# A hybrid decoder layer: a partial sum of squares on VectorE, and tokens made one by one, in the opening

## The chip, the core and the metric

The kernel runs on one core of a Trainium2 chip. The metric is the device time of one execution in microseconds. The core has TensorE (PE in the profile; its weight loads are PEld), VectorE (DVE), ScalarE (ACT), GpSimd (POOL) and SyncE (SP), which here issues the loads and stores.

## The reference

One layer: adaLN modulation, a mixer (sliding-window attention beside a Mamba-2 scan), a SwiGLU network, float32, 2048 positions of width 1024. The opening of the kernel computes only what stands here, for the first 512 positions:

```python
mod = jax.nn.silu(c) @ w_ada[layer] + b_ada[layer]
shift1, scale1, gate1, shift2, scale2, gate2 = jnp.split(mod, N_MOD, axis=-1)
h = modulate(rmsnorm(x, norm1_w[layer]), shift1, scale1)   # h * (1 + scale) + shift
proj = h @ w_in                                            # here: the q, k, v and dt columns
```

## The kernel before, in words

The width of 1024 lies on the partitions as 8 blocks of 128, called d or k. A tile of x, `x0[d]`, is 128 (one block of the width) by 512 (positions). The positions are worked in four blocks of 512. "Token d" below is the finished operand h[d] of the first block, a pair of tiles: a high part rounded to fp32r, made on ScalarE, and a low part, the rest, made on VectorE. A weight tile is split in the same way, and a product of the two is three matmuls (`mm3`, L286 to L288).

`opening()` makes the first block's operands and its projections to queries (all 512 positions) and to keys, values and dt (256 positions).

- Sum of squares (L1376, L1378): ScalarE squares each `x0[d]`, TensorE multiplies each square by ones and adds over d in one bank, 4 matmuls of two columns per d, 32 in all. The page counts each f32 matmul as two instructions.
- Root and spread: `root_of` computes 1/rms per position on VectorE in twelve small steps, `diagonal` (L331) puts it on four diagonals, and the matmul in `spread` (L337) copies it to all partitions, into the bank `bc`.
- Modulation: for most d the two numbers per partition (scale, shift) come from rows of `w_ada`: two loads of 512 KB (`rows_of`) and two reduces on VectorE against `csil` (L1395), then `scl1` (L1398). For two of the d they come from TensorE: eight products of the silu of c with blocks of `w_ada` (`ada_loads`, `ada_products`, L175), copied by ScalarE as one line and turned into columns by small matmuls (`ada_columns`, L180 to L186).
- `pair_ready(kp, raws)`: makes two tokens and the three split weights (two for the queries, one for keys, values and dt) of one pair kp of blocks d. L1416 scales on VectorE, L1418 and L1423 are the token's high and low part, L1413, L1420, L1422 and L1424 those of the weights.
- `first_columns(h)` is a generator: each `next(main)` issues the 30 matmuls of one k.
- `silu_rows` and `silu_columns` make silu(c) as rows (`csil`) and as columns (`ccol`); `rope_angles` and `rope_tables` make the cosines and sines of the first block.

The whole of `opening()` stands in a `manual_schedule` for TensorE, VectorE, SyncE and ScalarE: these queues take its instructions in the order of the text. What follows is ordered by a planner at build time, which may queue an instruction of the following text between those of the opening, wherever it finds it ready. That holds for L1474 to L1476: the exponential `neg_a` on ScalarE, which needs the small load `row`, and two VectorE steps. The low parts of the next weights (L279) are held behind the opening's last VectorE instruction (`pair_done`).

Behind the opening come `drain(main)` (rotary embedding of what `first_columns` summed: L402 to L405, dt at L482), the keys and values of the other 256 positions, then the convolutions (L499 to L514) and the norm of the second block (`norm1`, L341 to L344, L368).

Buffers that matter here: 5 raw weight tiles (`RAW`) and 6 split ones (`SPLIT`), 8 temporaries (`TMP`), four row tiles in each of `common.m4` and `extra.m4`, four banks `dense()` and four side banks.

Of the kernel before, what the change touches and what calls it, by code (L numbers as in the profile page):

```python
# [12 lines left out]
F32 = mybir.dt.float32  # L13
# [32 lines left out]
def hymba_layer(ctx, tc, xT, xtok, pos, wada, wadk, vecs, rows, wq, wkv, wz, wx, wo, wgu, wd, outT):  # L46
# [24 lines left out]
    def side_bank(i):  # L71
        return bank(("am", "at", "sm", "st")[i], 1)

    def tmp():
        return big("t", TMP, pool=fw)
# [70 lines left out]
    csil = const([P, D], "csil", pool=ip)  # L146

    def silu_rows():
        for i in range(2):
            dg, bk = tmp(), side_bank(i)  # L150
            for j in range(4):
                nc.vector.tensor_scalar(dg[:, j * P:(j + 1) * P], ident, ccol[:, 4 * i + j:4 * i + j + 1], 0.0,
                                        ALU.mult, ALU.add)
            nc.tensor.matmul(bk, ones, dg, start=True, stop=True)
            nc.scalar.copy(csil[:, i * T:(i + 1) * T], bk)

    def silu_columns():
        th = tmp()[:, 0:KT]
        nc.scalar.activation(th, ccol, AF.Tanh, scale=0.5)
        nc.vector.scalar_tensor_tensor(ccol, th, 1.0, ccol, ALU.add, ALU.mult)  # L160
# [1202 lines left out]
    def opening():  # L1363
        h, x0 = [], []
        for d in range(KT):
            x = extra.m2()
            x0.append(x)
            nc.sync.dma_start(x, xT[0, d])
        silu_columns()
        silu_rows()  # L1370
        nc.vector.tensor_copy(posf, posi)
        angles = rope_angles(0, NT)
        st = side_bank(2)
        for d in range(KT):
            sq = tmp()
            nc.scalar.activation(sq, x0[d], AF.Square)  # L1376
            for t in range(NT):
                nc.tensor.matmul(st[:, 2 * t:2 * t + 2], sq[:, t * P:(t + 1) * P], ones[:, 0:2], start=d == 0 and t == 0,  # L1378
                                 stop=d == KT - 1 and t == NT - 1, skip_group_check=True)
        rope_tables(angles)  # L1380

        def fetched(kp):
            raws = [wt.tile([P, 528], F32, name="raw", tag="raw", bufs=RAW)[:, 0:n] for n in (T, T, 528)]
            for raw, src in zip(raws, (wq[0][kp], wq[1][kp], wkv[kp])):
                fetched.last = nc.sync.dma_start(raw, src)
            return raws

        def rows_of(d, tile):
            got = [tile().rearrange("p h t -> p (h t)").bitcast(F32) for _ in range(2)]
            for w, i in zip(got, (8 + d, d)):  # L1390
                nc.sync.dma_start(w, wada[i])
            return got

        def reduced(i, w):
            nc.vector.tensor_tensor_reduce(w, w, csil, 0.5, b_ada[:, i:i + 1], ALU.mult, ALU.add, mod[:, i:i + 1])  # L1395

        def scale_of(d):
            nc.vector.scalar_tensor_tensor(scl1[:, d:d + 1], mod[:, 8 + d:9 + d], 1.0, n1w[:, d:d + 1],  # L1398
                                           ALU.add, ALU.mult)

        def vectors(d, rows):
            reduced(8 + d, rows[0])
            reduced(d, rows[1])
            scale_of(d)

        def pair_ready(kp, raws):

            ds, ws, xs = (2 * kp, 2 * kp + 1), [], []
            for raw in raws:
                two = wt.tile([P, 2, 528], F32R, name="w", tag="w", bufs=SPLIT)  # L1410
                ws.append((two[:, 0, 0:raw.shape[1]], two[:, 1, 0:raw.shape[1]]))
            for i in range(2):
                nc.scalar.activation(ws[i][0], raws[i], AF.Copy)  # L1413
            for d in ds:
                x = tmp()
                nc.vector.scalar_tensor_tensor(x, x0[d], scl1[:, d:d + 1], bc, ALU.mult, ALU.mult)  # L1416
                h.append(operand())
                nc.scalar.activation(h[d][0], x, AF.Identity, bias=sh1[:, d:d + 1])  # L1418
                xs.append(x)
            nc.scalar.activation(ws[2][0], raws[2], AF.Copy)  # L1420
            for i, d in enumerate(ds):
                nc.vector.tensor_tensor(ws[i][1], raws[i], ws[i][0].bitcast(F32), ALU.subtract)  # L1422
                nc.vector.scalar_tensor_tensor(h[d][1], xs[i], sh1[:, d:d + 1], h[d][0].bitcast(F32), ALU.add, ALU.subtract)  # L1423
            last = nc.vector.tensor_tensor(ws[2][1], raws[2], ws[2][0].bitcast(F32), ALU.subtract)  # L1424
            pair_done[0] = last
            first_ws.append(ws)

        rows0, rows1 = rows_of(0, common.m4), rows_of(1, common.m4)
        nc.sync.dma_start(row, rows.broadcast_to([P, 32]))
        raws = [fetched(0)]  # L1430
        spare = []
        for _ in range(4):
            taken[0] += 1
            spare.append(ip.tile([P, 2, T], F32R, name="hl0", tag="hl0", bufs=4).bitcast(F32))
        first = ada_loads(0, spare)
        rows4, rows5 = rows_of(4, extra.m4), rows_of(5, extra.m4)
        line = side_bank(0)
        reduced(8, rows0[0])
        bc = spread(root_of(st, NT), bc=side_bank(1))
        reduced(0, rows0[1])  # L1440
        scale_of(0)
        ada_products(first, line, range(8))
        vectors(1, rows1)
        main = first_columns(h)
        pair_ready(0, raws[0])
        raws.append(fetched(1))
        rows6, rows7 = rows_of(6, common.m4), rows_of(7, common.m4)
        next(main)
        vectors(4, rows4)
        vectors(5, rows5)  # L1450
        ada_columns(line, side_bank(0), 2)
        next(main)
        pair_ready(1, raws[1])
        raws.append(fetched(2))
        next(main)
        next(main)
        pair_ready(2, raws[2])
        raws.append(fetched(3))
        next(main)
        next(main)  # L1460
        vectors(6, rows6)
        vectors(7, rows7)
        pair_ready(3, raws[3])
        next(main)
        next(main)
        return h, main, fetched.last

# [292 lines left out]
def _layout(x, c, positions, w_ada, b_ada, norm1_w, w_in, conv_w, conv_b, dt_bias, a_log, d_skip, attn_sinks,  # L1760
            ssm_norm_w, w_out, norm2_w, w_gate_up, w_down, final_norm_w):
    a = np.ascontiguousarray
    out = {}
    out["xT"] = a(x[0].T.reshape(KT, P, NB, T).transpose(2, 0, 1, 3))
    out["xtok"] = a(x[0].reshape(S // P, P, 2, T).transpose(0, 2, 1, 3))
    out["pos"] = a(positions[0].reshape(S // P, P).T)
    out["wada"] = a(w_ada[0].T.reshape(48, P, D))
    wk = w_ada[0].reshape(D, 6, 4, 2 * P)
    out["wadk"] = a(np.stack([np.concatenate([wk[:, 1, 1], wk[:, 0, 1]], axis=1)])
                    .reshape(1, 4, 2, P, T).transpose(0, 1, 3, 2, 4).reshape(1, 4, P, 2 * T))  # L1770
    cols = lambda v, n: v.reshape(n, P).T
    cw = conv_w[0].reshape(4, 8, P).transpose(2, 1, 0).reshape(P, 32)
    out["vecs"] = a(np.concatenate([cols(b_ada[0], 48), cols(norm1_w[0], 8), cols(norm2_w[0], 8),
                                    cols(final_norm_w, 8), cw, cols(conv_b[0], 8), cols(ssm_norm_w[0], 4), cols(c[0], 8)], axis=1))
    sk = attn_sinks[0].reshape(2, 4).T.reshape(8)
    out["rows"] = a(np.concatenate([dt_bias[0], a_log[0], d_skip[0], sk])[None])
    w = w_in[0]
    q = w[:, 0:512].reshape(D, 2, 4, 64).transpose(0, 2, 1, 3).reshape(D, 512)

    def moving(m, n):  # L1780
        return m.reshape(4, 2, P, -1, n).transpose(3, 0, 2, 1, 4).reshape(-1, 4, P, 2 * n)

    out["wq"] = a(moving(q, 256))
    out["wkv"] = a(moving(np.concatenate([w[:, 512:768], w[:, 2304:2312]], axis=1), 264)[0])
    out["wz"] = a(moving(w[:, 768:1280], 256))

    def chunks(m, n):
        return m.reshape(2, 4, P, n, P).transpose(3, 0, 2, 1, 4).reshape(n, 2, P, 512)

    out["wx"] = a(chunks(w[:, 1280:2304], 8))  # L1790
    wo = w_out[0]
    attn = wo[0:512].reshape(2, 4, 64, D).transpose(1, 0, 2, 3).reshape(512, D)
    out["wo"] = a(chunks(np.concatenate([attn, wo[512:]], axis=0), 8))
    gu = w_gate_up[0]
    out["wgu"] = a(np.stack([chunks(gu[:, :FF], NF), chunks(gu[:, FF:], NF)], axis=1))
    out["wd"] = a(w_down[0].reshape(KP, 2, P, 8, P).transpose(3, 1, 2, 0, 4).reshape(8, 2, P, KP * P))
    return out
# [20 lines left out]
```

## Time and profile before

| | |
|---|---|
| median of 3 runs | 2178.56 us (2177.98 to 2180.01) |
| profiled execution | 2179.79 us, span 2177.7 us |
| mean granted TensorE clock | 0.997 |
| TensorE, VectorE, ScalarE, GpSimd busy | 98%, 76%, 47%, 25% |
| DMA | 466.76 MB, mean 214 GB/s |

A busy time is the share of the span in which the engine had an instruction of the program at work; a wait is idle time and what ended it. TensorE's matmuls overlap, so its costs are read from start to start.

### The profile page before, as it was taken

Reading aid. Unit: us, or ns where it says so; the run is one execution under the profiler, and the core shown is the slowest. Engines: PE = TensorE matmul, PEld = TensorE weight load, DVE = VectorE, ACT = ScalarE, POOL = GpSimd, SP = SyncE. Lnnn points to the kernel's source line nnn. Section 1 sums busy time; section 2 is a strip of 40 time slices with the busy share of each in tenths; the row PEclk is TensorE's granted clock in tenths of the full one; section 3 lists DMA queues with packets and bytes.
Section 4 is the critical chain, followed back from the end, with each engine's and each line's share of the span. In section 5 each row is a group of like instructions: output and inputs, shape, how many; then the busy total and the mean of one; then the engine's idle time right before and its main releaser. Section 6 shows DMA issues by size and latency. Waiting matters only on the chain.

```text
span 2177.7 us, 33314 instructions
## 1 busy us (share of the span) xinstructions
PE 2139.7 (98%) x10984; PEld 1764.9 (81%) x10984; DVE 1651.1 (76%) x3195; ACT 1016.5 (47%) x2137; POOL 553.5 (25%) x658
## 2 busy tenths in 40 slices
PE   8989999999999999999999999999999999999998
PEld 6889898879778777788888878788888888888887
DVE  6987857885778866798897678777877765886576
ACT  3675735653557454433344445433333334554441
POOL 0223433322112211243441212333333331210011
PEclk9999999999999999999999999999999999999999
DMA  7798978797998332333335778645555536778553
GB/s 269 237 341 297 353 260 312 255 342 238 360 357 313 109 97 92 121 109 124 115 94 178 248 244 293 216 155 187 166 167 179 168 112 232 239 266 278 184 161 105
DMA packets 287708, 466.76 MB, mean 214 GB/s; under 512 B 27440, under 2 KB 97072, under 8 KB 287536
## 3 DMA queue, kind: packets, MB, share of 16 engines
q1 hardware_dynamic: 286960, 464.13, 63.3%
q8 instruction: 86, 1.41, 0.3%
q14 instruction: 86, 0.70, 0.1%
q10 hardware_dynamic: 576, 0.52, 0.1%
HBM read 329.73 MB, written 134.81 MB: 213 GB/s over the span
## 4 chain that ended last, share of the span: by engine, by line
PE 79%; DVE 8%; DMA 5%; ACT 3%; issue 2%; POOL 1%; SPq 0%; DVEq 0%; ACTq 0%; POOLq 0%
PE d L1182 17%; PE d L1052 9%; PE d L1051 9%; PE d L1050 9%; PE d L286 4%; PE d L287 4%; PE d L288 4%; DMA aw<-in_wada_dram 1%; PE d L1323 1%; PE am L1050 1%; PE am L1052 1%; PE am L1051 1%; PE am L706 1%; PE sm L1052 1%; PE sm L1051 1%
## 5 line engine op out<-in xcount | busy, mean ns | idle before, releaser
L1182 PE MATMUL d<-a,w 128*128 128x512 f32 x1716 | 403.5, 396 | 2.2 <-DVE a L1164 2.2
L1182 PEld LDWEIGHTS d<-a,w 128*128 128x128 f32 x1716 | 323.2, 189 | 79.6 <-DVE a L1164 2.9
L1052 PE MATMUL d<-b,w 128*128 128x512 f32 x924 | 366.9, 399 | 0.6 <-DVE w L898 0.6
L1051 PE MATMUL d<-b,w 128*128 128x512 f32 x924 | 366.6, 397 | 0.7 <-DVE b L932 0.5
L1050 PE MATMUL d<-b,w 128*128 128x512 f32 x924 | 363.2, 397 | 0.0
L897 ACT ACTIVATE w<-s 128x512 fp32r<-128x512 f32 x176 | 111.0, 631 | 237.2 <-PE d L1052 148.2
L1051 PEld LDWEIGHTS d<-b,w 128*128 128x128 f32 x924 | 174.2, 189 | 41.7 <-DVE b L932 1.5
L1052 PEld LDWEIGHTS d<-b,w 128*128 128x128 f32 x924 | 173.8, 188 | 40.4 <-DVE w L898 1.0
L1050 PEld LDWEIGHTS d<-b,w 128*128 128x128 f32 x924 | 174.2, 189 | 38.0
L286 PE MATMUL d<-w,hl 128*128 128x256 f32 (+1 forms) x592 | 171.9, 290 | 2.7 <-DVE s L511 2.7
L287 PE MATMUL d<-w,hl 128*128 128x256 f32 (+1 forms) x592 | 166.9, 282 | 0.0
L288 PE MATMUL d<-w,hl 128*128 128x256 f32 (+1 forms) x592 | 166.8, 282 | 0.0
L1178 DVE TENSOR_TENSOR w<-raw,w 128x512 fp32r<-128x512 f32 x156 | 114.0, 739 | 43.3 <-ACT w L1177 43.0
L1104 POOL TENSOR_TENSOR t<-t 128x512 f32<-128x512 f32 x44 | 75.5, 1717 | 277.0 <-DVE t L1103 126.1
L1164 DVE TENSOR_TENSOR a<-a 128x512 fp32r<-128x512 f32 x154 | 106.2, 704 | 46.1 <-ACT a L1163 45.3
L898 DVE TENSOR_TENSOR w<-s,w 128x512 fp32r<-128x512 f32 x176 | 131.1, 746 | 6.3 <-ACT w L897 5.4
L1163 ACT ACTIVATE a<-a 128x512 fp32r<-128x512 f32 x154 | 96.1, 629 | 85.1 <-DMA a<-act_t 50.1
L296 POOL TENSOR_TENSOR acc<-acc,t 128x512 f32<-128x512 f32 x35 | 51.8, 1481 | 325.7 <-ACT t L295 312.1
L286 PE MATMUL d<-hl,w 128*128 128x512 f32 x320 | 131.6, 411 | 0.0
L288 PE MATMUL d<-hl,w 128*128 128x512 f32 x320 | 126.1, 394 | 0.0
L1177 ACT ACTIVATE w<-raw 128x512 fp32r<-128x512 f32 x156 | 90.6, 587 | 75.8 <-PE d L1182 44.3
L287 PE MATMUL d<-hl,w 128*128 128x512 f32 x320 | 125.7, 393 | 0.0
(426 smaller groups left out, 4802.6 us busy)
## 6 DMA issues: line engine op xcount, KB each, us to landing
raw<-in_wgu_dram SPq DMA_DIRECT2D x176, 256.0 KB, 3.0
act_t<-t SPq DMA_DIRECT2D x88, 256.0 KB, 2.9
a<-act_t SPq DMA_DIRECT2D x88, 256.0 KB, 4.5
act_b<-t SPq DMA_DIRECT2D x66, 256.0 KB, 2.0
a<-act_b SPq DMA_DIRECT2D x66, 256.0 KB, 4.2
aw<-in_wada_dram SPq DMA_DIRECT2D x64, 256.0 KB, 5.1
w<-w_x SPq DMA_DIRECT2D x32, 512.0 KB, 5.5
raw<-wd_s SPq DMA_DIRECT2D x64, 256.0 KB, 3.2
```

Of the source, the lines that this page charges most:

```text
L286: nc.tensor.matmul(out, ahi, bhi, start=first, stop=False)
L287: nc.tensor.matmul(out, ahi, blo, start=False, stop=False)
L288: mm3.last = nc.tensor.matmul(out, alo, bhi, start=False, stop=last)
L897: nc.scalar.activation(hi, x, AF.Copy)
L898: eng.tensor_tensor(lo, x, hi.bitcast(F32), ALU.subtract)
L1050: nc.tensor.matmul(out, ahi, bhi, start=first and k == 0, stop=False, skip_group_check=True)
L1051: nc.tensor.matmul(out, ahi, blo, start=False, stop=False, skip_group_check=True)
L1052: mm3.last = nc.tensor.matmul(out, alo, bhi, start=False, stop=k == 3, skip_group_check=True)
L1163: nc.scalar.activation(hi, raw, AF.Copy)
L1164: nc.vector.tensor_tensor(lo, raw, hi.bitcast(F32), ALU.subtract)
L1178: nc.vector.tensor_tensor(w[1], raw, w[0].bitcast(F32), ALU.subtract)
L1182: mm3.last = nc.tensor.matmul(ps, w[x][:, ws], act[k][y], start=new and k == 0 and x + y == 0, stop=k == KP - 1 and x == 1, skip_group_che ...
```

## The change

- Sums: the squares of blocks 0, 1 and 2 go to TensorE as before. The square of block 3 is written into an accumulator tile, VectorE adds those of 4 to 7 to it, and TensorE sums the accumulator: 16 matmuls instead of 32.
- The two copies that end `silu_rows` are issued behind the squares of blocks 2 and 4.
- Loads: all of the opening's first loads are issued ahead of `silu_columns`. Behind x come the four blocks for the products, rows 0, the small `row`, the weights of pair 0, rows 3, two of the three weights of pair 1, rows 4 and 5; the third weight of pair 1 and rows 6 follow token 0.
- The products serve blocks 1 and 2 (before: 2 and 3); rows serve 0 and 3 to 7. Four products stand ahead of the spread, four behind it. `ada_columns` stands ahead of the first `next(main)`.
- Tokens: `pair_ready` is gone; `scaled_token` (scaling and high part), `closed` (low part), `high` and `low` (weights) stand one by one behind the reduces of their own rows.

```diff
     def silu_rows():
+        copies = []
...
-            nc.scalar.copy(csil[:, i * T:(i + 1) * T], bk)
+            copies.append(lambda i=i, bk=bk: nc.scalar.copy(csil[:, i * T:(i + 1) * T], bk))
+        return copies
...
+        early = ada_loads(0, spare)
+        rows0 = rows_of(0, common.m4)
+        nc.sync.dma_start(row, rows.broadcast_to([P, 32]))
+        raw0 = fetched(0)
+        rows3 = rows_of(3, extra.m4)
+        raw1 = fetched(1, (0, 1))
+        rows4, rows5 = rows_of(4, extra.m4), rows_of(5, common.m4)
+
+        silu_columns()
+        copies = silu_rows()
+        nc.vector.tensor_copy(posf, posi)
+        angles = rope_angles(0, NT)
+        st, acc = side_bank(2), sums()
...
+        for d in range(KT):
+            sq = acc if d == 3 else tmp()
+            nc.scalar.activation(sq, x0[d], AF.Square)
+            if d in (2, 4):
+                copies[d // 2 - 1]()
+            if d < 3:
+                summed(sq, d == 0, False)
+            elif d > 3:
+                nc.vector.tensor_tensor(acc, acc, sq, ALU.add)
+        rope_tables(angles)
+        summed(acc, False, True)
+
         line = side_bank(0)
-        reduced(8, rows0[0])
-        bc = spread(root_of(st, NT), bc=side_bank(1))
-        reduced(0, rows0[1])
-        scale_of(0)
-        ada_products(first, line, range(8))
-        vectors(1, rows1)
+        dg = diagonal(root_of(st, NT))
+        ada_products(early, line, range(4))
+        bc = spread(None, bc=side_bank(1), dg=dg)
+        ada_products(early, line, range(4, 8))
+        vectors(0, rows0)
+        w0 = high(raw0)
+        low(raw0, w0, (0,))
+        x = scaled_token(0)
+        low(raw0, w0, (1, 2))
+        closed(*x)
+        raw1 += fetched(1, (2,))
+        rows6 = rows_of(6, common.m4)
+        first_ws.append(w0)
+        vectors(3, rows3)
         main = first_columns(h)
-        pair_ready(0, raws[0])
-        raws.append(fetched(1))
-        rows6, rows7 = rows_of(6, common.m4), rows_of(7, common.m4)
+        ada_columns(line, side_bank(0), 1)
         next(main)
-        vectors(4, rows4)
-        vectors(5, rows5)
-        ada_columns(line, side_bank(0), 2)
-        next(main)
-        pair_ready(1, raws[1])
-        raws.append(fetched(2))
+
+        xs = [scaled_token(d) for d in (1, 2)]
+        w1 = high(raw1)
+        closed(*xs[0])
+        low(raw1, w1, (0,))
+        closed(*xs[1])
+        low(raw1, w1, (1, 2))
+        raw2, rows7 = fetched(2), rows_of(7, extra.m4)
+        first_ws.append(w1)
         next(main)
         next(main)
-        pair_ready(2, raws[2])
-        raws.append(fetched(3))
+
+        x = scaled_token(3)
+        vectors(4, rows4)
+        closed(*x)
         next(main)
+        x = scaled_token(4)
+        w2 = high(raw2)
+        low(raw2, w2, (0,))
+        closed(*x)
+        low(raw2, w2, (1, 2))
+        raw3 = fetched(3)
+        first_ws.append(w2)
         next(main)
+        vectors(5, rows5)
+        x = scaled_token(5)
         vectors(6, rows6)
+        closed(*x)
+        next(main)
+        x = scaled_token(6)
+        w3 = high(raw3)
+        low(raw3, w3, (0,))
+        closed(*x)
+        low(raw3, w3, (1, 2))
+        first_ws.append(w3)
+        next(main)
         vectors(7, rows7)
-        pair_ready(3, raws[3])
-        next(main)
+        closed(*scaled_token(7))
         next(main)
```

More of the change, by code (lines that the diff above doesn't have):

```diff
@@ L1368, in opening, with fetched @@
             nc.sync.dma_start(x, xT[0, d])
[L1369 to L1385, printed above, removed]
+        def fetched(kp, which=(0, 1, 2)):
+            raws = [wt.tile([P, 528], F32, name="raw", tag="raw", bufs=RAW)[:, 0:(T, T, 528)[i]] for i in which]
+            for raw, i in zip(raws, which):
+                fetched.last = nc.sync.dma_start(raw, (wq[0], wq[1], wkv)[i][kp])
             return raws
@@ L1392, in rows_of, with vectors, high @@
             return got
-        def reduced(i, w):
-            nc.vector.tensor_tensor_reduce(w, w, csil, 0.5, b_ada[:, i:i + 1], ALU.mult, ALU.add, mod[:, i:i + 1])
-        def scale_of(d):
+        def vectors(d, loaded):
+            for w, i in zip(loaded, (8 + d, d)):
+                nc.vector.tensor_tensor_reduce(w, w, csil, 0.5, b_ada[:, i:i + 1], ALU.mult, ALU.add, mod[:, i:i + 1])
             nc.vector.scalar_tensor_tensor(scl1[:, d:d + 1], mod[:, 8 + d:9 + d], 1.0, n1w[:, d:d + 1],
                                            ALU.add, ALU.mult)
[L1401 to L1408, printed above, removed]
+        def high(raws):
+            ws = []
             for raw in raws:
@@ L1411, in pair_ready, with low, scaled_token, closed @@
                 ws.append((two[:, 0, 0:raw.shape[1]], two[:, 1, 0:raw.shape[1]]))
[L1412 to L1430, printed above, removed]
+                nc.scalar.activation(ws[-1][0], raw, AF.Copy)
+            return ws
+        def low(raws, ws, which):
+            for i in which:
+                pair_done[0] = nc.vector.tensor_tensor(ws[i][1], raws[i], ws[i][0].bitcast(F32), ALU.subtract)
+        def scaled_token(d):
+            x = tmp()
+            nc.vector.scalar_tensor_tensor(x, x0[d], scl1[:, d:d + 1], bc, ALU.mult, ALU.mult)
+            hl = operand()
+            nc.scalar.activation(hl[0], x, AF.Identity, bias=sh1[:, d:d + 1])
+            return d, x, hl
+        def closed(d, x, hl):
+            pair_done[0] = nc.vector.scalar_tensor_tensor(hl[1], x, sh1[:, d:d + 1], hl[0].bitcast(F32),
+                                                          ALU.add, ALU.subtract)
+            h.append(hl)
         spare = []
@@ L1434, in opening @@
             spare.append(ip.tile([P, 2, T], F32R, name="hl0", tag="hl0", bufs=4).bitcast(F32))
-        first = ada_loads(0, spare)
-        rows4, rows5 = rows_of(4, extra.m4), rows_of(5, extra.m4)
-        line = side_bank(0)
-        reduced(8, rows0[0])
-        bc = spread(root_of(st, NT), bc=side_bank(1))
-        reduced(0, rows0[1])
-        scale_of(0)
-        ada_products(first, line, range(8))
-        vectors(1, rows1)
+        early = ada_loads(0, spare)
+        rows0 = rows_of(0, common.m4)
@@ new lines, in opening, with summed @@
+        nc.sync.dma_start(row, rows.broadcast_to([P, 32]))
[8 more added lines that the diff above has]
+        st, acc = side_bank(2), sums()
+        def summed(sq, first, last):
+            for t in range(NT):
+                nc.tensor.matmul(st[:, 2 * t:2 * t + 2], sq[:, t * P:(t + 1) * P], ones[:, 0:2], start=first and t == 0,
+                                 stop=last and t == NT - 1, skip_group_check=True)
@@ L1767, in _layout @@
     out["wada"] = a(w_ada[0].T.reshape(48, P, D))
-    wk = w_ada[0].reshape(D, 6, 4, 2 * P)
-    out["wadk"] = a(np.stack([np.concatenate([wk[:, 1, 1], wk[:, 0, 1]], axis=1)])
+    wk = w_ada[0].reshape(D, 6, D)[:, :, P:3 * P]
+    out["wadk"] = a(np.stack([np.concatenate([wk[:, 1], wk[:, 0]], axis=1)])
                     .reshape(1, 4, 2, P, T).transpose(0, 1, 3, 2, 4).reshape(1, 4, P, 2 * T))
```

## The prediction

> **What bounds the kernel now.** I read the page first, then the waits of TensorE, then the stretch up to 130 us in order of time, engine by engine, and last the loads with their landings.
>
> ```profile
> PE 2139.7 (98%) x10984; PEld 1764.9 (81%) x10984; DVE 1651.1 (76%) x3195; ACT 1016.5 (47%) x2137; POOL 553.5 (25%) x658
> ```
>
> TensorE is busy for 98% of the span, so only what shortens its work or its idle time moves the end. Of its waits in the first 110 us the view has three; this is the one the change touches most:
>
> ```profile
> PE at L337 <- DVE t L331: 3.3, 1, 3.3
> ```
>
> The opening in order of time (start, length, engine, line, tiles, count). Consecutive instructions overlap, so I take a cost from start to start.
>
> ```profile
> 8.95 4.26 ACT L1376 ACTIVATE t<-m 128x512 f32<-128x512 f32 x8
> 9.47 0.23 DVE L241 TENSOR_SCALAR m<-m 128x128 f32<-128x128 f32 x1
> 9.64 13.81 PE L1378 MATMUL sm<-ones,t 128*128 128x2 f32 x64 [1.21 <-ACT t L1376]
> 17.08 0.17 DVE L1475 TENSOR_SCALAR neg_a<-neg_a 128x8 f32<-128x8 f32 x1 [3.63 <-ACT neg_a L1474]
> 23.49 0.16 DVE L309 TENSOR_SCALAR ms<-sm 128x4 f32<-128x4 f32 x1 [6.24 <-PE sm L1378]
> 25.86 0.87 DVE L331 TENSOR_SCALAR t<-ident,rstd 128x128 f32<-128x128 f32 x4
> 26.79 2.07 PE L337 MATMUL at<-t,ones 128*128 128x512 f32 x2 [3.34 <-DVE t L331]
> 28.79 7.95 PE L175 MATMUL am<-hl,vec 128*1 128x512 f32 x16
> 36.67 0.39 PE L286 MATMUL d<-w,hl 128*128 128x256 f32 x1
> 36.83 0.58 ACT L180 COPY t<-am 1x512 f32<-1x512 f32 x1 [3.73 <-PE am L175]
> 40.45 1.05 PE L182 MATMUL am<-ones,t 1*128 1x2 f32 x8
> 41.43 0.39 PE L286 MATMUL d<-w,hl 128*128 128x256 f32 x1
> 46.40 1.39 DVE L1416 SCALAR_TENSOR_TENSOR t<-m,scl,at 128x512 f32<-128x512 f32 x2
> 50.87 1.27 DVE L1395 CUSTOM_DVE_ANT_0 m<-m,csil,vec 128x1024 f32<-128x1024 f32 x1
> 55.84 1.39 DVE L1416 SCALAR_TENSOR_TENSOR t<-m,scl,at 128x512 f32<-128x512 f32 x2
> 60.30 1.32 DVE L279 TENSOR_TENSOR w<-raw,w 128x528 fp32r<-128x528 f32 x2
> 66.63 0.28 PE L287 MATMUL am<-w,hl 128*128 128x264 f32 x1
> ```
>
> The reader sees one chain: squares, sums on TensorE (13.8 us), root and diagonal on VectorE, the spread, eight products L175, and at 36.67 the first projection matmul. From there TensorE never waits: token-row 0 takes 36.67 to 40.45, the column turn L182 1.0, and the other seven run from 41.43 to 66.63, 25.2/7 = 3.6 us each. VectorE ends the opening at 60.30. Its rates: two tokens with one weight pair take 50.87-46.40 = 4.47 us, two modulation rows with their scales 55.84-50.87 = 4.97 divided by two, 2.49 for one d (two reduces and a scale).
>
> **The change, part by part.**
>
> *Sums.* 64 instructions in 13.81 us are 0.216 each. Tokens 0 to 2 stay, and the accumulator is a fourth: 32 instead of 64, 6.9 us of TensorE removed. The squares go ahead of the two silu copies, so the sums can start when TensorE's silu products end (8.4, where the 1.2 us idle time before 9.64 began). Three rows of sums take 5.2 us, to 13.6.
>
> *The adds.* VectorE adds four squares into the fifth. The last x lands late:
>
> ```profile
> m<-in_xT_dram SPq DMA_DIRECT2D x1, 256.0 KB, 5.7
> L1422 DVE TENSOR_TENSOR w<-raw,w 128x512 fp32r<-128x512 f32 x8 | 5.5, 683 | 0.0
> L1423 DVE SCALAR_TENSOR_TENSOR hl<-t,mod,hl 128x512 fp32r<-128x512 f32 x8 | 5.9, 743 | 0.0
> L296 POOL TENSOR_TENSOR acc<-acc,t 128x512 f32<-128x512 f32 x35 | 51.8, 1481 | 325.7 <-ACT t L295 312.1
> ```
>
> Issued at 5.0, it lands at 10.7; its square (0.53 each by 4.26/8) is done at 11.3. VectorE is through with the angles at 9.7 (L241), so three adds fit ahead of that square and one follows. An f32 add of this shape stands on VectorE in no row of the opening; I take 0.68 by L1422, its nearest row, and bound it by nothing and by GpSimd's 1.48. So the accumulator is ready at 12.2, before TensorE wants it at 13.6; at 1.48 each, four from 9.7, it would be 15.6 and the sums would end 1.9 us later. With 0.68 they end at 13.6+1.7 = 15.4 against 23.45: 8 us earlier. An add that cost nothing would gain nothing, since TensorE is busy until 13.6.
>
> *The clock of the sums.* The loads of the sums are slow from first to last:
>
> ```profile
> L1378 PEld LDWEIGHTS sm<-ones,t x64: 288/333/333, 9.6 to 23.0; 128*128 128x128 f32 x64
> ```
>
> So I keep 0.216 for what remains. The Trainium skill ("TensorE: Matmul & The Clock Gate", Part 1) says that sustained work of some 3.4 us doubles the array's rate. By it the removed 32 would be worth 32 x 0.108 = 3.5 us, and the whole sum below 3.5 instead of 6.9. The row contradicts it for matmuls of two columns: 13 us of them without a pause, and the median load is the longest one. So the sum goes by the row.
>
> *Spread and products.* Root and diagonal take 23.49 to 26.79, 3.3 us: done at 18.7. Four products, moved ahead of the spread, fill that time, if their blocks have landed (below: 13.3). Half of L175's 7.95 and L337's 2.07 put the spread's end at 21.4, the other half the last product's at 25.4. TensorE's 3.3 us wait goes.
>
> *The column turn* is moved ahead of the first tokens: ScalarE's copy (0.58), covered before by token 0's matmuls, is now bare, then L182's 1.0: first projection matmul at 27.0, 9.7 us earlier, and the 1.0 that stood between tokens 0 and 1 is gone. Token 0 would end at 30.6, and with VectorE keeping up TensorE would be 10.7 us ahead. VectorE does not keep up, as its walk below shows.
>
> *Loads.* The queue and two landings (from issue):
>
> ```profile
> 5.51 2.92 SPq L1391 DMA_DIRECT2D m<-in_wada_dram  x4
> 8.76 0.37 SPq L1429 DMA_DIRECT2D row<-in_rows_dram  x1
> 20.14 1.61 SPq L1385 DMA_DIRECT2D raw<-in_wq_dram  x2
> m<-in_wada_dram SPq DMA_DIRECT2D x1, 512.0 KB, 6.5
> row<-in_rows_dram SPq DMA_DIRECT2D x1, 16.0 KB, 8.1
> raw<-in_wq_dram SPq DMA_DIRECT2D x1, 256.0 KB, 8.9
> ```
>
> The first 512 KB behind x land at 12.0; each 512 KB more takes 1.3 us. In the new order: the four blocks for the products 12.0 to 15.6, rows 0 at 18.2, the small rows at 19.6 (16.9 before, plus two blocks), first weights 20.2 to 21.6, rows 3 about 24, weights kp 1's first two 25.4, rows 4 and 5 at 30.4, as before. The third load of kp 1 waits on SP for the first raw buffer, free when VectorE has made that weight's low part (21.8); behind it on SP wait rows 6, kp 2, rows 7, kp 3. The queue is still eight us deep then, so nothing runs dry, and this load lands at about 31.1.
>
> *VectorE, in its order.* Rows 0 from 18.7 to 21.2; token 0 with its weights (a token 1.32, a weight trio 1.82: the 4.47 divided by the lengths 0.74 and 0.69) to 24.3; rows 3 to 26.8; the turned columns 0.4. Tokens 1 and 2 with kp 1 cost 4.47, plus 0.7 of waiting for ScalarE and the load of 31.1: 32.4. Then five tokens (6.6), two weight trios (3.6), four d's rows (9.9): 20.2. ScalarE runs in order too, and the new text puts a token's high part ahead of the weight's:
>
> ```profile
> L1418 ACT ACTIVATE hl<-t,mod 128x512 fp32r<-128x512 f32 x8 | 5.5, 724 | 22.2 <-DVE t L1416 22.2
> L1413 ACT ACTIVATE w<-raw 128x512 fp32r<-128x512 f32 x8 | 4.7, 622 | 2.8 <-issue 2.3 <-DMA raw<-in_wq_dram 0.5
> ```
>
> VectorE therefore waits 0.72+0.62 = 1.35 at kp 2 and again at kp 3, and 0.72 at token 7: 3.4. The opening ends on VectorE at 32.4+20.2+3.4 = 56.0, 4.3 ahead of 60.30. This is what is late next: VectorE has token 5 at 47.0, token 6 with its weights at 51.5 and token 7 at 56.0, while TensorE, at 3.6 a token from 27.0, is free for them at 45.0, 50.6 and 55.1. It idles 2.0+0.9+0.9 us. Token 7 runs 56.0 to 59.6, against 66.63: 7.0 earlier. Were the 3.4 us of VectorE's waits not there, it would be 10.4.
>
> The edits with one answer: rows are reduced for 0 and 3 to 7 instead of 0, 1 and 4 to 7, and the columns turned are those of 1 and 2 instead of 2 and 3, so the count of reduces (12), of turns and of bytes loaded is the same, and the other layout of the products' blocks costs nothing; one of the reduces, done before in the idle time ahead of the root, now follows it and is in the walk.
>
> *Behind the opening.*
>
> ```profile
> 60.30:66.10 5.80, 5.80 (x51) 5.80 (x50) 3.12 (x7) 5.15 (x17) 0.00 (x0) 1.00 0.87 292
> 72.30:108.00 35.70, 35.70 (x156) 28.99 (x155) 35.63 (x91) 24.47 (x41) 13.24 (x19) 1.00 0.76 244
> 71.06 0.23 DVE L482 TENSOR_TENSOR dt<-d,row 128x8 f32<-128x8 f32 x2
> 72.34 0.39 PE L286 MATMUL d<-hl,w 128*128 128x512 f32 x1
> 127.58 0.39 PE L286 MATMUL d<-w,hl 128*128 128x256 f32 x1 [2.73 <-DVE s L511]
> ```
>
> VectorE (fourth column) is full from 72 to 108 and TensorE runs into it at 127.58, so its lead counts. It gains 4.3 by its own work, and between 60.30 and 66.10 it idled 2.7 us for TensorE's token 7; with token 7 closer behind, that idling goes. 4.3+2.7 = 7.0, the same as TensorE's 7.0. The first convolution needs a bank that L482 frees (71.3 against 72.34): about a microsecond of slack, which holds.
>
> **Sum.** 7.0 us, less 0.1 for rounding on that seam: 6.9. The profiled execution took 2179.79 (span 2177.7 and 2.1 around it), 1.2 above the median of 2178.56; so 2172.9 for it and 2171.7 for the median.
>
> **Rivals.**
>
> *The small rows hold VectorE.* L1475 needs them; it stands behind the opening in the text but was queued ahead of the root (17.08 before 23.49). Queued there again, it waits for the landing at 19.6 and ScalarE's exponential: the root starts at 20.0 instead of 15.4, and all of VectorE moves 4.5. Against it: sums would now end well before that landing, which the planner may see. Gain 2.4: 2176.2.
>
> *Only VectorE's own lead arrives,* because its idling before 66 stays or returns as a wait near 127: gain 4.3, 2174.3. For it: 35.63 of 35.70 busy.
>
> *More:* the 3.4 us of waits behind ScalarE are not there, because ScalarE has split the weights by the time VectorE asks: gain 10.3, 2168.3. Against it: its queue is in the order of the text.
>
> *Slower: an eviction behind the next norm.* The rest is planned anew. VectorE makes block 1's tokens in bunches:
>
> ```profile
> 113.75 3.11 DVE L341 SCALAR_TENSOR_TENSOR t<-t,scl,bc 128x512 f32<-128x512 f32 x3
> 116.88 2.73 DVE L341 SCALAR_TENSOR_TENSOR t<-t,scl,bc 128x512 f32<-128x512 f32 x4
> ```
>
> A convolution's eviction queued behind both waits 5.8 us, and TensorE with it for want of a bank. To come out 0.2% slower the loss must pass 6.9+4.4 = 11.3, which two evictions so placed do: 2171.7+11.7 = 2183.4. One leaves 2177.5, no change. Against it: the only such wait now is 2.73.
>
> **How the numbers follow.** 0.2% (4.4 us) is about what a measurement of this kernel tells from none. Forecast 0.52, more 0.10, VectorE's lead alone 0.15 (at the boundary, so a quarter of it counted as faster), small rows 0.13, slower 0.10. Faster 0.52+0.10+0.04 = 0.66, same 0.11+0.13 = 0.24, slower 0.10. The range takes in both ends of the unknown add (1.9 us, 2173.6; nothing instead of 0.68 gains none) and all rivals but the slower one: 2168 to 2177. The likeliest case alone: 2169.5 to 2174.
>
> **What the new profile would show.** The sums as 32 instructions ending near 15.4; L309's successor right behind; products on both sides of the spread; first projection matmul near 27.0; TensorE idle 4 us before tokens 5 to 7, released by VectorE; the opening's end on VectorE near 56, on TensorE near 59.6; the convolutions near 65.3. L1475 ahead of the root would prove the first rival. Wrong I would be if rows 0 or the first weights land later than 21.6, or if TensorE's waits between 66 and 150 us grow by what the opening saved.

## The result: slower, 2184.04 us against 2178.22

| | before | after |
|---|---|---|
| median of 13 runs each | 2178.22 us (2174.26 to 2180.23) | 2184.04 us (2177.01 to 2189.75) |
| ratio, 95% interval | | 1.0025 [1.0015, 1.0036] |
| profiled execution | 2179.79 us, span 2177.7 | 2177.74 us, span 2175.4 |
| mean granted TensorE clock | 0.997 | 0.994 |

The profiled execution of the changed kernel is one of its shortest, 6.3 us under its median; that of the kernel before is 1.6 over its own. This pair of traces ends 2.05 us earlier for the changed kernel, so it shows where a lead goes and not the whole loss; medians and traces are kept apart below.

The opening did what was forecast. First the page's line of engines, then TensorE in order of time (start, length, engine, line, tiles, count, the wait ahead of it):

```profile
PE 2134.2 (98%) x10952; PEld 1757.9 (81%) x10952; DVE 1661.2 (76%) x3199; ACT 1013.0 (47%) x2137; POOL 558.4 (26%) x658
```

```profile
7.60 2.74 PE L1434 MATMUL sm<-ones,t 128*128 128x2 f32 x24
12.97 1.86 PE L1434 MATMUL sm<-ones,acc 128*128 128x2 f32 x8 [2.64 <-DVE acc L1445]
14.77 5.03 PE L177 MATMUL am<-hl,vec 128*1 128x512 f32 x8
19.72 1.13 PE L339 MATMUL at<-t,ones 128*128 128x512 f32 x2
25.09 1.05 PE L184 MATMUL am<-ones,t 1*128 1x2 f32 x8 [0.72 <-ACT t L182]
...
47.77 0.39 PE L290 MATMUL d<-w,hl 128*128 128x256 f32 x1 [1.89 <-DVE hl L1410]
...
122.73 0.38 PE L288 MATMUL d<-w,hl 128*128 128x256 f32 x1 [3.94 <-DVE s L513]
```

The sums end at 14.8 instead of 23.45, the products stand on both sides of the spread, the first projection matmul follows the column turn at 26.1. The last row answers to the one at 127.58 of before: there TensorE waits for the same eviction, 3.9 us instead of 2.7, and is 4.85 us early. VectorE of the same kernel:

```profile
9.63 0.69 DVE L1445 TENSOR_TENSOR acc<-acc,t 128x512 f32<-128x512 f32 x1 [0.38 <-ACT t L1439]
10.63 2.29 DVE L1445 TENSOR_TENSOR acc<-acc,t 128x512 f32<-128x512 f32 x3 [0.31 <-ACT t L1439]
14.87 0.16 DVE L311 TENSOR_SCALAR ms<-sm 128x4 f32<-128x4 f32 x1 [1.96 <-PE sm L1434]
20.45 0.17 DVE L1515 TENSOR_SCALAR neg_a<-neg_a 128x8 f32<-128x8 f32 x1
38.73 0.69 DVE L1400 TENSOR_TENSOR w<-raw,w 128x512 fp32r<-128x512 f32 x1 [1.31 <-ACT w L1395]
56.31 0.75 DVE L1410 SCALAR_TENSOR_TENSOR hl<-t,mod,hl 128x512 fp32r<-128x512 f32 x1 [0.79 <-ACT hl L1406]
56.98 1.94 DVE L281 TENSOR_TENSOR w<-raw,w 128x528 fp32r<-128x528 f32 x3
```

VectorE starts the next weights' low parts, its first work behind the opening, at 56.98 instead of 60.30: 3.3 us early, beside TensorE's 6.

To see where a lead goes, one needs the same work in both traces. The spread of `1/rms` (L337 before, L339 after) is such a marker: few instructions, once for each norm, the tile's name telling which. The view groups instructions by line and tile; its columns are the count, the duration of one (shortest, median, longest) and the start of the first and of the last. Before, then after:

```profile
L337 PE MATMUL st<-t,ones x12: 377/592/593, 637.3 to 2156.3; 128*128 128x512 f32 x10, 128*128 128x256 f32 x2
L337 PE MATMUL d<-t,ones x6: 590/592/593, 108.5 to 373.9; 128*128 128x512 f32 x6
...
L337 PE MATMUL am<-t,ones x2: 592/644/697, 1302.4 to 1302.9; 128*128 128x512 f32 x2
```

```profile
L339 PE MATMUL st<-t,ones x12: 377/592/593, 632.4 to 2153.8; 128*128 128x512 f32 x10, 128*128 128x256 f32 x2
L339 PE MATMUL d<-t,ones x6: 590/592/593, 102.4 to 370.5; 128*128 128x512 f32 x6
...
L339 PE MATMUL am<-t,ones x2: 593/645/697, 1302.0 to 1302.5; 128*128 128x512 f32 x2
```

The lead is 6.1 us at 108.5, 3.4 at 373.9, 4.9 at 637.3 and 0.4 at 1302.4. The changed code ends at 60 us; 2.7 of the 6.1 us go in the next 270 us, and 4.5 between 637 and 1302 us, where the kernel's text is the same.

What differs there is the order. Both programs have the same instructions behind the opening, but the planner puts them into the queues anew: of TensorE's 10239 places 1206 hold another instruction than before, all between about 700 and 1250 us; VectorE's queue differs in 536 places of 2900, ScalarE's in 283 of 1915, SyncE's in 179 of 1648, GpSimd's in 27 of 612. The first quarter of the queues holds 181 of VectorE's differences, 67 of ScalarE's, 71 of SyncE's and none of TensorE's.

### The profile page after: what moved, and what is told of

It reads as the page before. It is cut to its first block, busy times and chain, and to the rows that moved or that the text cites. A ratio compares the mean times of both kernels' runs of the same rounds, so it can differ in the third digit from the quotient of the medians.

```text
span 2175.4 us, 33233 instructions
## 1 busy us (share of the span) xinstructions
PE 2134.2 (98%) x10952; PEld 1757.9 (81%) x10952; DVE 1661.2 (76%) x3199; ACT 1013.0 (47%) x2137; POOL 558.4 (26%) x658
## 4 chain that ended last, share of the span: by engine, by line
PE 78%; DVE 9%; DMA 7%; ACT 3%; issue 2%; SPq 1%; POOL 0%; DVEq 0%; ACTq 0%; POOLq 0%
PE d L1184 15%; PE d L1054 9%; PE d L1052 9%; PE d L1053 9%; PE d L288 6%; PE d L290 5%; PE d L289 5%; PE d L1325 1%; PE am L1052 1%; PE am L1054 1%; PE am L1053 1%; PE am L708 1%; PE sm L1054 1%; PE sm L1053 1%; DMA t<-in_xT_dram 1%
## 5 line engine op out<-in xcount | busy, mean ns | idle before, releaser
L1166 DVE TENSOR_TENSOR a<-a 128x512 fp32r<-128x512 f32 x154 | 109.1, 721 | 55.9 <-ACT a L1165 55.3
```

The costliest lines, as they stand in the source:

```text
L1166: nc.vector.tensor_tensor(lo, raw, hi.bitcast(F32), ALU.subtract)
```

## The experiments

The theory: (a) the opening brings a gain, but only VectorE's lead of it arrives; (b) the new order of the rest costs more than that. Its rival: the parts of the opening themselves (the adds, or the tokens) cost later what they bring. "Before" below is a run of the kernel before on the same chip: 2177.33, 2177.72 and 2178.2 us in the three groups of runs.

**The changed kernel again**, twice timed, and once more for its trace only (no edit).

> The changed kernel unaltered, to get the trace of a second execution: the one shown ends 0.5 us under before's median while its median is 5.8 us above. Theory A (TensorE's clock: behind the opening it now falls to half for stretches of 3.4 us, more in some executions than in others): an execution of 2184 us or more shows more such stretches than the two the first trace has between 110 and 160 us, its granted clock is 0.993 or lower, and the loss against the first trace sits at those stretches. Rival B (loads or stores that land later in some executions): the clock is the same within 0.001 and the extra time sits in TensorE's waits for DMA.

> The same kernel a second time, for one more trace. Theory A: time and granted clock go together, about 2.2 us for each 0.001 of the clock. Rival B: no relation. If this execution and the one before differ by under 2 us they can be averaged and nothing is told apart.

> The change once more for a trace: the three so far ended at 2177.7, 2180.6 and 2178.8 while the median of the untraced ones is near 2184. If this one is at 2183 or above, the place of the missing 4 us shows as steps against the other traces: as half-clock stretches by the theory of the clock (about 2 us for each 0.001), as waits for DMA by its rival. At 2178 to 2180 it tells nothing.

Measured: 2182.11 (2178.71 to 2190.56), ratio 1.0026 [1.0013, 1.0039]; 2182.42 (2178.79 to 2188.71), 1.0028 [1.0016, 1.0041]; the third trace is of an execution of 2180.86. The loss repeats. The traced executions lie at 2180.55, 2178.79 and 2180.86; none is as long as the 2183 or more at which they were to tell the clock from the loads, so that question was not answered.

**One part alone.** `sums_only` is before with the accumulator and the moved silu copies; `tokens_only` is after with all eight sums on TensorE:

```diff
 sums_only, against before:
-            sq = tmp()
+            sq = acc if d == 3 else tmp()
...
+            if d in (2, 4):
+                copies[d // 2 - 1]()
+            if d < 3:
+                summed(sq, d == 0, False)
+            elif d > 3:
+                nc.vector.tensor_tensor(acc, acc, sq, ALU.add)
...
+        summed(acc, False, True)
 tokens_only, against after:
-            if d < 3:
-                summed(sq, d == 0, False)
-            elif d > 3:
-                nc.vector.tensor_tensor(acc, acc, sq, ALU.add)
+            summed(sq, d == 0, d == KT - 1)
...
-        summed(acc, False, True)
```

> Before, with the sums alone changed: five squares added on VectorE, the silu copies behind squares 2 and 4; loads and tokens as before. The root should start near 15 us instead of 23.5 and the first projection matmul be held by the products' blocks, which land at 24.2, so near 29 instead of 36.7. Theory A: 7 us gained at the first convolution (72.34 before), and the end 4 us earlier to 4 us later, by what the planner makes of the rest. Rival C (the rest passes on whatever the opening gains, and it is the new token order that costs): 2172.

> The change without the accumulator: all eight squares summed on TensorE, tokens and loads as in the change. The sums run at 0.114 us each in the trace of the change, so 64 end near 15 or, at 0.216, near 21.5; then the opening is 0 to 6 us later than in the change. Theory A: the end lies within 2178 to 2188, not ordered by the opening. Rival C: 0 to 6 us above the change, 2184 to 2190.

Measured: `sums_only` 2174.46 (2169.99 to 2177.16), 0.9981 [0.9972, 0.9991]: faster. `tokens_only` 2187.89 (2181.62 to 2190.76), 1.0041 [1.0028, 1.0054]: slower, and within the ranges of both theories. Their sums on TensorE, and the work behind them, `sums_only` first:

```profile
8.22 5.12 PE L1379 MATMUL sm<-ones,t 128*128 128x2 f32 x24
13.20 1.85 PE L1379 MATMUL sm<-ones,acc 128*128 128x2 f32 x8
```

```profile
7.69 10.64 PE L1434 MATMUL sm<-ones,t 128*128 128x2 f32 x64
18.26 5.05 PE L177 MATMUL am<-hl,vec 128*1 128x512 f32 x8
...
60.84 1.94 DVE L281 TENSOR_TENSOR w<-raw,w 128x528 fp32r<-128x528 f32 x3
```

The sums are the part that gains: 15.05 instead of 23.45 in the old token order, 14.77 instead of 18.26 in the new. The new tokens alone bring VectorE nothing: its opening ends at 60.84, 0.5 later than before. But each of these two kernels got a plan of its own for the rest, so the parts are not yet told apart from the plan. (A new plan need not cost anything: that of `sums_only` differs from before's in 2183 of TensorE's places, and the kernel is the faster one.)

**The order held.** Edges between neighbours of each queue fix the order without a wait on the chip; ORDER lists, for each of the five queues, the program order that another kernel has behind its opening:

```diff
+        rest_from = len(nc.cur_bb.bb.instructions)      # end of opening()
...
+    made, at = nc.cur_bb.bb.instructions[rest_from:], 0
+    for _ in range(5):
+        turns = ...                                     # one queue of ORDER
+        for a, b in zip(turns, turns[1:]):
+            tc.add_manual_dep(made[b], made[a].name, mybir.DependencyInfo(
+                mybir.DependencyClass.NoSync, mybir.DependencyReason.DATA), reason="order")
```

`after_old_order` is the changed opening with before's order behind it, `before_new_order` before's opening with the changed kernel's order, `sums_old_order` is `sums_only` in before's order.

> The changed kernel, its opening as it is, and everything behind the opening queued on all five engines in the order that before's program has (17,314 instructions; in the change 1206 places of TensorE's queue, 536 of VectorE's, 283 of ScalarE's, 179 of SyncE's differ from it). Theory A' (the loss is the new order of the rest): the 3.7 us lost between 700 and 1400 us and part of the 2.3 lost between 120 and 150 come back: 2172 to 2176. Rival B' (the rest waits in any order, because loads, ScalarE and VectorE behind the opening were not earlier, and TensorE's clock falls while it waits): 2181 to 2184 as the change.

> Before with its own opening, and the rest queued in the order of the changed kernel's program. Theory A': as much slower than before as the new order costs, 5 to 11 us: 2183 to 2189. Rival B': no change, 2176 to 2180. If it is slower by about 4 us the order is half of it.

> The kernel with the sums alone changed (2174.5, first convolution 7.2 us earlier), the rest in before's order. Its own plan differs from before's in 2183 places of TensorE's queue. Theory A': the order of before passes on what the opening gains, so 2170 to 2173. Rival B': the loss does not lie in the order, 2174 to 2176 as before.

> Before itself once more, for a second trace: the differences between traces are so far taken against a single one. If its progress at 160, 360, 650 and 1400 us lies within 1 us of the first trace, the steps read so far are the kernels'; if it wanders by 3 us, the steps at 340 us (1.3 to 5.3 us lost in the traces so far) are chance of one execution.

Measured: `after_old_order` 2176.5 (2174.96 to 2185.07), 0.9996 [0.9987, 1.0006]; `before_new_order` 2189.75 (5 runs, 2183.89 to 2190.28), 1.0047 [1.0034, 1.0059]; `sums_old_order` 2175.01 (2168.63 to 2181.16), 0.9986 [0.9976, 0.9995]; `before_again` one execution of 2179.66. With the opening of before and nothing changed but the order, the kernel is slower by 0.47%, 10 us (12 by the medians): the order alone suffices. With the old order the changed kernel's loss is gone, 5.6 us under its own median in the runs of the first group. `sums_old_order` missed its forecast: 2175.01 lies in the range of the rival (2174 to 2176), so the old order did not pass on to the end what the sums gain. That the edges themselves slow a kernel is not seen: `after_old_order` and `sums_old_order` have them and are not slower than before. No run holds before in its own order by edges.

The markers of `before_new_order`, then of `after_old_order` (their L455 and L457 are L337 of before):

```profile
L455 PE MATMUL st<-t,ones x12: 377/592/593, 643.2 to 2166.0; 128*128 128x512 f32 x10, 128*128 128x256 f32 x2
L455 PE MATMUL d<-t,ones x6: 590/592/697, 107.6 to 380.6; 128*128 128x512 f32 x6
...
L455 PE MATMUL am<-t,ones x2: 592/644/697, 1313.6 to 1314.1; 128*128 128x512 f32 x2
```

```profile
L457 PE MATMUL st<-t,ones x12: 377/592/593, 633.7 to 2153.4; 128*128 128x512 f32 x10, 128*128 128x256 f32 x2
L457 PE MATMUL d<-t,ones x6: 590/592/593, 102.5 to 370.9; 128*128 128x512 f32 x6
...
L457 PE MATMUL am<-t,ones x2: 592/592/592, 1298.6 to 1299.0; 128*128 128x512 f32 x2
```

From 637 to 1302 before takes 665.1 us; the old order behind the new opening 664.9, the new order behind the old opening 670.4. That kernel is 0.9 us early at 108.5 and 6.7 late at 373.9, so more than half of its loss falls ahead of this stretch.

**Early or late.** In `late_old` only the last three quarters of each queue are held in before's order, the first quarter is the kernel's own; in `early_old_late_new` it is the other way round. Both have the changed opening.

> The change, with the last three quarters of each engine's queue (behind some 450 us) in before's order and the first quarter as the change's own plan has it. Theory: the traces lose 2.7 to 4.1 us between 690 and 1300 us under the new order and nothing under the old one, so 3 to 5 us below the change: 2178 to 2180. Rival: the cost of the new order lies in the first 150 us (181 places of VectorE's queue, 67 of ScalarE's, 71 of SyncE's): no gain, 2182 to 2184.

> The other half: the change with the first quarter of each queue in before's order and the rest in the change's own. Theory: 3 to 5 us above the change with all of the old order (2176.5): 2180 to 2182. Rival: 2176.5. If both halves lie half way the two add.

Measured: `late_old` 2177.87 (2172.12 to 2182.08), 0.9999 [0.9989, 1.0009]; `early_old_late_new` 2181.63 (2179.13 to 2187.42), 1.0021 [1.0012, 1.003]. The changed kernel's loss goes with the late part. From the same three rows of each trace:

| kernel | late order | 108.5 | 373.9 | 637.3 | 1302.4 | from 637 to 1302 |
|---|---|---|---|---|---|---|
| before, before_again | old | 0, -0.2 | 0, -0.1 | 0, +0.9 | 0, +1.4 | 665.1, 665.6 |
| after_old_order | old | -6.0 | -3.0 | -3.6 | -3.8 | 664.9 |
| late_old | old | -6.0 | +1.4 | +1.8 | +2.4 | 665.7 |
| sums_old_order | old | -7.8 | -7.1 | -7.5 | -6.9 | 665.7 |
| weights_first_old | old | -8.7 | -5.2 | -5.2 | -4.5 | 665.8 |
| sums_only | its own | -7.2 | -1.5 | -2.5 | -2.8 | 664.8 |
| after | new | -6.1 | -3.4 | -4.9 | -0.4 | 669.6 |
| again_1 | new | -5.7 | 0.0 | -0.6 | +2.4 | 668.1 |
| again_2 | new | -5.1 | -2.7 | -3.5 | +1.0 | 669.6 |
| again_3 | new | -6.3 | -5.0 | -3.4 | +1.6 | 670.1 |
| early_old_late_new | new | -4.5 | -3.1 | -3.8 | +0.4 | 669.3 |
| before_new_order | new | -0.9 | +6.7 | +5.9 | +11.2 | 670.4 |
| tokens_only | its own | -2.1 | -0.3 | +0.8 | +4.4 | 668.7 |

(Columns three to six: start of the marker that before has at that time, less that time, in us.) The last column falls into two groups, 664.8 to 665.8 and 668.1 to 670.4, whatever the opening: the six traces with the new order average 669.5, the six with the old one 665.5, 4.0 us less. Of the 4.0, 0.7 come back behind 1302: to the last st marker the new order takes 852.0 on average, the old one 852.7. By the medians, each less that of before in its own group of runs, the late order costs 3.4 + 1.2 = 4.6 us (`early_old_late_new` against `after_old_order`) or 4.8 + 0.3 = 5.1 (`again_1` against `late_old`), the early one about 1. From 640 to 1400 us the waits of TensorE (line, what it waited for, us in total, times, longest) are, after and then `after_old_order`:

```profile
PE d L1053 <- DVE b L934: 1.4, 2, 1.2
PE sm L820 <- ACT m L740: 1.1, 1, 1.1
PE d L1184 <- DVE a L1166: 1.1, 1, 1.1
PE am L699 <- DVE ast L674: 1.1, 1, 1.1
PE am L339 <- DVE t L333: 0.8, 1, 0.8
...
```

```profile
PE d L1302 <- DVE a L1284: 2.7, 2, 2.2
PE am L817 <- DVE ast L792: 1.1, 1, 1.1
PE d L1172 <- DVE w L1018: 0.6, 1, 0.6
PE d L1171 <- DVE b L1052: 0.5, 1, 0.5
...
```

The new order has waits that the old one lacks: for b (1.4 instead of 0.5), for m of L740, which is not in the second list, and for the diagonal of the next norm. From marker to marker, without the waits for `a` (L1166, L1284), which lie behind it, the whole lists add up to 6.2 and 2.7 us: 3.5 of the 4.7 between these two traces. But waits alone do not part the two groups, for `weights_first_old`, in the old order, waits 5.0 us there and takes 665.8.

VectorE's work does part them. The stretch from marker to marker (its length, then busy time and count of PE, PEld, DVE, ACT and POOL, granted clock, DMA share, GB/s) and one group of VectorE's instructions in it (count, busy time, mean ns of one, idle time before), after and then `after_old_order`:

```profile
632.40:1302.00 669.60, 662.75 (x3239) 533.94 (x3237) 531.69 (x900) 310.69 (x678) 182.68 (x199) 1.00 0.48 158
L729 DVE TENSOR_TENSOR m<-upper,ahi 128x512 fp32r<-128x512 f32 x16 | 17.1, 1072 | 4.9 <-PE sm L738 4.9
```

```profile
633.70:1298.60 664.90, 662.00 (x3239) 535.47 (x3238) 524.25 (x900) 313.50 (x679) 180.12 (x199) 1.00 0.49 159
L847 DVE TENSOR_TENSOR m<-upper,ahi 128x512 fp32r<-128x512 f32 x16 | 13.4, 845 | 3.5 <-PE sm L856 3.5
```

The same 900 instructions keep VectorE busy for 530.4 to 531.9 us in the six traces with the new order and for 523.9 to 525.2 in the six with the old one. In that stretch 669 of them are TENSOR_TENSOR or SCALAR_TENSOR_TENSOR with an output of 128x512. Most take about 0.7 us; those over 0.9 (up to 1.8) are 75 or 76 in the new order and 67 to 69 in the old, and in all twelve traces each of these runs while GpSimd is at work on an instruction, against about a quarter of the short ones. So the new order makes VectorE's work longer where it falls beside GpSimd's. That GpSimd is what lengthens it, and how much of TensorE's 4 us comes of it, is argued from these counts and was not tried.

**More lead for VectorE.** If VectorE's lead is what arrives, then taking away its waits for ScalarE must pass on one to one. The split of the weights goes ahead of the token, in the old order:

```diff
+        w2 = high(raw2)
         x = scaled_token(4)
-        w2 = high(raw2)
...
+        w3 = high(raw3)
         x = scaled_token(6)
-        w3 = high(raw3)
```

> The change with the rest in before's order, and in the opening ScalarE splits the weights of pairs 2 and 3 ahead of tokens 4 and 6, so that VectorE's two waits of 1.3 us go and it leaves the opening 2.6 us earlier; TensorE leaves it about as much earlier. Theory (behind the opening the rest goes at VectorE's lead, 3.4 us, not at TensorE's 6.0, until TensorE has waited the difference off at 125 us): 2176.5 less 2 to 2.6, 2174. Rival (what is lost at 125 us is lost to the stores of the convolutions, which ScalarE waits 3.6 us for): 2176 to 2177.

Measured: 2173.11 (2170.74 to 2180.44), 0.9981 [0.9971, 0.9991]. It is faster than both kernels, with `sums_only` at the same ratio. VectorE's two rows that tell its lead are the end of the opening and the eviction for which TensorE waits in the first convolutions; `before` (its first is the prediction's row at 60.30), `after_old_order`, `weights_first_old`, `sums_old_order`:

```profile
126.78 0.74 DVE L511 SCALAR_TENSOR_TENSOR s<-d,vec,s 128x512 f32<-128x512 f32 x1
```

```profile
56.91 1.32 DVE L399 TENSOR_TENSOR w<-raw,w 128x528 fp32r<-128x528 f32 x2
...
123.36 0.74 DVE L631 SCALAR_TENSOR_TENSOR s<-d,vec,s 128x512 f32<-128x512 f32 x1
```

```profile
54.19 1.32 DVE L399 TENSOR_TENSOR w<-raw,w 128x528 fp32r<-128x528 f32 x2
...
120.70 0.74 DVE L631 SCALAR_TENSOR_TENSOR s<-d,vec,s 128x512 f32<-128x512 f32 x1
```

```profile
52.50 1.32 DVE L399 TENSOR_TENSOR w<-raw,w 128x528 fp32r<-128x528 f32 x2
...
119.02 0.74 DVE L631 SCALAR_TENSOR_TENSOR s<-d,vec,s 128x512 f32<-128x512 f32 x1
```

VectorE leads by 3.39, 6.11 and 7.80 us at the end of the opening, and by 3.42, 6.08 and 7.76 at the eviction. In these three its lead passes 65 us of full work unchanged, and TensorE's larger lead (6.0 and 8.7 in the first two) is cut down to it. A fourth kernel with the old early order, `early_old_late_new`, is less exact: 3.31 (56.99) become 4.03 (122.75), with 4.5 for TensorE.

To the end of the typical run the lead does not pass in full: by the medians the three gain 1.2, 5.1 and 2.7 us for leads of 3.39, 6.11 and 7.80. The rival, that the adds or the tokens cost later what they bring, is contradicted for the adds by the trace of `sums_old_order`, which keeps its lead to the end (2147.2 for the last st marker, 9.1 us early), but that execution is 4.2 us under the kernel's median; by the median it is still open where 5 of the 7.8 us go. For the tokens without the adds it was not tried in the old order.

## Why the prediction was wrong

*Right, in mechanism and nearly in size.* The root at 14.87 (forecast 15.4), first projection matmul at 26.1 (27.0), VectorE's waits for ScalarE 1.31 twice and 0.79 (1.35 twice and 0.72), TensorE's waits ahead of tokens 5 to 7 3.4 (3.8), VectorE's end 56.98 (56.0), TensorE's lead behind the opening, at the marker of 108.5, 6.1 (7.0). The adds take 0.69 each, forecast 0.68. The first rival, the small rows ahead of the root, did not come: L1515 stands at 20.45, behind it.

*The clock of the sums, mis-sized without effect.* The prediction kept 0.216 us a matmul. In the changed kernel's trace the first 24 took 2.74, 0.114 each, and TensorE then stood 2.6 us for VectorE's accumulator. The Trainium skill ("TensorE: Matmul & The Clock Gate", Part 1), whose rule the prediction set aside, says that the array warms after some 3.4 us of work, and that the count of cold matmuls changes from run to run because the window runs freely. The traces agree with the second: the same kernel's 24 sums took 2.74 in one execution and 5.12 in another (`again_2`). The first they do not show for these two-column sums, and there the prediction read its row rightly: in before 64 of them in 13.81 us without a pause stayed at 0.216. In `tokens_only`, whose 64 follow the 512-column products without a pause, 11 ran in each us until 11 us and 6 in each from there to their end at 18, with a granted clock of 1.00 and then 0.50. So in no trace did the sums make the array faster, and here they did not keep it fast either. The removed 32 were worth 18.26 - 14.77 = 3.5 us with the new tokens and 23.45 - 15.05 = 8.4 with the old, of which 1.4 by the earlier start (8.22 instead of 9.64). Slow or fast, the sums end near the accumulator's arrival, so the root did not move by it.

*The step that failed: "Behind the opening".* "4.3+2.7 = 7.0, the same as TensorE's 7.0" took VectorE's idle time behind the opening for gained. In the old order nothing of it was: the lead that arrives at the eviction is VectorE's own, 3.4 for this opening (one trace with the old early order shows 0.7 more). That is the mechanism of the second rival, which had chance 0.15. In the new order the eviction at 121.94 is 4.84 early, and in the three other traces of the same kernel 3.8, 3.7 and 5.8, so part of the idle time goes, but then another cost follows: TensorE's longer wait (3.9) is followed by a stretch in which the granted clock reads 0.50. Ten us around it, with the columns as above; before, then after:

```profile
120.00:130.00 10.00, 7.27 (x60) 6.86 (x58) 10.00 (x19) 6.83 (x17) 3.28 (x4) 1.00 0.87 288
```

```profile
120.00:130.00 10.00, 7.27 (x52) 6.98 (x53) 9.88 (x22) 6.49 (x15) 7.12 (x6) 0.83 1.01 359
```

A mean of 0.83 over 10 us is 3.4 us at half clock. Of 4.85 us at 122.73, 3.5 are left at 156 (the same matmuls in both traces); a second such stretch lies at 143, behind a wait of 1.8, and before has a wait of 2.0 for a DMA there, so the price of the first alone is not told.

*The order of the rest, taken for harmless.* The fourth rival said "The rest is planned anew" and was right in that; its place was wrong. It looked for a wait of 5.8 us at the first convolutions, and there the wait is 3.9. The cost lies between 640 and 1300 us, far from the edited text, and is 4.0 us by the traces and 4.6 to 5.1 by the medians; VectorE is busy 7 us longer there with the same instructions. The prediction had no term for an order that changes where no text does.

*The account.* Forecast 6.9 us. VectorE's lead alone leaves 3.4. With the order held, 2177.72 - 2176.5 = 1.2 are measured; the interval of that ratio ends at a gain of 2.8, so 3.4 lies just outside it and some of VectorE's lead is lost behind the eviction. Where is open: the markers between 108 and 374 show a loss that changes from one execution to the next: identical kernels stand at 3.4, 0.0, 2.7 and 5.0 us of lead at 374. With the kernel's own order it is 2182.11 - 2177.33 = 4.8 slower: 6.0 for the order.

*What stays open.* The four traced executions of the changed kernel (2177.74 to 2180.86) lie up to 6.3 us under its medians, so its typical run loses something that no trace shows. In its 33 timed runs the time rises as the granted clock falls, from 2178.98 at 0.996 to 2187.83 and 2190.56 at 0.990; whether the lower clock is the cause or follows from more waits was not tried. Against the clock as the cause: in before's 83 timed runs, at 0.989 to 0.998, the time does not rise as the clock falls, and `after_old_order` reads 0.994 in its median and is as fast as before. At the end of the traces the order's price is hardly seen either: the traced executions of the changed kernel and of `after_old_order` are 2177.74 and 2177.41.

## What to carry to other kernels

A gain in one stage passes on only as far as the engine leads on which the next stage waits: take that engine's end as the most that can pass, and count no idle time as won until a row shows what fills it. Where a planner orders the rest, an edit of the opening is two changes, and they can be told apart by holding one order for both openings and by giving the old opening the new order. Markers that occur once in each phase, such as a norm's spread, show in which stretch a lead is lost, where a list of waits shows only a part; the busy time of each engine between two markers then shows whose work grew longer.

## What was not expected of the hardware

- The page's granted clock reads 1.00 from 5 to 10 us both where the sums run at 0.114 us each (after) and where they run at 0.213 (`again_2`, 24 in 5.12), so at the start of these traces that column does not tell a slow array from a fast one; the durations do.
- After waits of TensorE of 3.6 us or more near 122 to 128 us half clock for 3.4 us or more followed in each trace that had one (after, `again_1`, `again_2`, `after_old_order`, `late_old`, `weights_first_old`, `tokens_only`, `before_new_order`). It also followed shorter ones with a second wait of about 1.5 us close behind (2.64 in `sums_only`, 2.77 in `sums_old_order`, 3.24 in `early_old_late_new`); after 2.73 in before, 2.65 in `before_again` and 3.26 in `again_3` none did.
- The order of instructions that are the same in number and kind, with no engine's busy share moved by more than one point, was worth 10 us (1.0047 [1.0034, 1.0059]) behind an opening of one and the same text.
